# The value tiles, the output transposes and half B's stream of a hybrid encoder, laid out and ordered differently

## The chip, the core and the metric

The kernel runs on one core of a Trainium2 chip, all in float32. The core has a matrix engine (TensorE, PE in the rows, with its weight loads as PEld), a vector engine (VectorE, DVE), a scalar engine (ScalarE, ACT), GpSimd (POOL) and SyncE (SP). Each engine works through its own instructions in the order in which they were laid down at build time. Transfers (DMAs) are issued by SP and by ACT and run on 16 shared DMA engines. The metric is the device time of one execution in microseconds (us).

## What is computed

A sequence of 1024 tokens with 1024 channels passes two mixing layers, each followed by a SwiGLU block, and a final norm. The part that matters here is the second layer, an RWKV-7 recurrence with 16 heads of 64:

```
def step(state, inp):                       # for each token
    r_t, w_t, k_t, v_t, a_t, b_t = inp
    sa = einsum('bhvk,bhk->bhv', state, a_t)
    state = state * w_t + sa[..., None] * b_t + v_t[..., None] * k_t
    return state, einsum('bhvk,bhk->bhv', state, r_t)
...
y = group_norm(y) * ln_w + ln_b             # per head
y = (y + sum(r * k * r_k) * v) * g          # bonus, gate
h = h + y @ w_o
...
h = h + (silu(hn @ w_gate) * (hn @ w_up)) @ w_down     # SwiGLU, both layers
```

## The kernel before

**Halves and precision.** The tokens are worked on in two halves of 512, A (h = 0) and B (h = 1). A dense product of float32 precision is made of three matmuls on split operands (`mm3`, L393 to L395): a weight is loaded into a tile `raw` (ACT issues it, L121), ScalarE writes its rounded part `whi` (L157), VectorE writes the rest `wlo` (L158). There are three `raw` buffers, used in turn.

**Order.** Instructions are not issued in the order of the source. A planner at build time gives every engine a fixed list: it takes whatever is ready by its own clock, lowest priority number first, and a priority is the instruction's place in the source. `drive(dense, side, ratio)` walks a dense product and a side task together: each piece of dense work lets the side run for `ratio` times its weight, in the units that the side yields. The side's instructions are given a place 450 instructions earlier (`tc.high_priority(offset=AHEAD)`, AHEAD = 450).

**The recurrence.** `recur(h, wp)` works on 8 chunks of 64 tokens per half. It is the side task of a SwiGLU stage: `ffn(0, 1, ..., D0P[:3])` at a ratio of 6.2 for half A, `ffn(1, 0, ..., G1A[1])` at a ratio of 3 for half B. `with_reload` wraps it and adds the reload of the residual stream `h` in four loads of 512 KB. Its parts:
- `load(c)` fetches a chunk's operands on SP: `ar` (L1471), `bk` (L1473), the values into `uv` (L1476, L1477) and two pieces of the inverse into `XT` (L1483, L1486). Both `load(0)` and `load(1)` stand at the start.
- `uv` is a tile of 128 partitions by 8 by 2 by 64; for each head parity r the values of 64 tokens fill one half of the partitions, and `burst` later writes the solution u into the other half (L1573, L1574).
- `lnw`, the norm's gain, is spread to all partitions by two loads that ACT issues ahead of everything (L1446).
- `burst(c, ...)` makes the chunk's products with small matmuls through three PSUM buffers named `sm`. All of the recurrence's PE instructions are chained by `ordered` (L1456), so on PE they keep the order of the source.
- `post(jj)`, after each odd chunk, takes the pair's output `yp` out of PSUM into `ysb` (L1623), makes the group norm on VectorE, ScalarE and GpSimd, multiplies by `lnw` (L1661), adds the bonus `vch` (L1662), and leaves a function `turn_out` behind. It also loads `gch` (gate, L1626) and `vch` (L1629).
- `turn_out` transposes `ysb` on PE through two `sm` buffers (8 transposes), combines it with the gate on VectorE in 8 instructions (L1678) and stores it to `y_d` on SP (L1681). Before the change it is called inside the next chunk's `burst`, behind `flip_bk` and ahead of `load(c + 2)`; the last pair's is called at the end.

Between two bursts `recur` yields 12 units (BURST = 12), 6 of them ahead of `post`. When half A's recurrence is through, `y_d` is loaded again, split (tiles `ahi`, `alo`) and multiplied by `w_o` in `out_proj(0, ...)`.

**Half B's stream.** Ahead of the recurrence stands the down projection of layer 0. Its last products of the stage before end, and then `H[0]` (pool `ha0`) and `H[1]` (pool `hb0`) are reloaded from `hm_d` on SP (L1873): two loads for A, four for B, 512 KB each. A side task `wa1` waits 8 units and then prepares two small weights. The first residual additions of the stage are at L908, the others at L487. The hidden tiles of the stage before are stored by L737 (`hid_d`) and loaded again by L888 (`hd`).

Of the kernel before, what the change touches and what calls it, by code (L numbers as in the profile page):

```python
# [11 lines left out]
AF = mybir.ActivationFunctionType  # L12
# [4 lines left out]
P = 128  # L17
D = 1024
T = 1024
KT = D // P  # L20
# [10 lines left out]
BURST = 12.0  # L31
# [12 lines left out]
def tile_trunk(  # L44
# [8 lines left out]
    act, dve, pool, pe, sp = nc.scalar, nc.vector, nc.gpsimd, nc.tensor, nc.sync  # L53
# [25 lines left out]
    def bc(ap, shape):  # L79
        return ap.to_broadcast(shape)  # L80
# [204 lines left out]
    hm_d = [dram.tile([P, KT, HT], F32, name=f"hm_d{h}") for h in range(2)]  # L285
# [78 lines left out]
    H = [hA, hB]  # L364
# [198 lines left out]
    for h in range(2):  # L563
        ops = [mmt() for _ in range(4)]
        for kp in range(4):
# [4 lines left out]
            for kk in range(2):  # L570
                k = 2 * kp + kk
# [497 lines left out]
    rows = [slice(0, 64), slice(64, 128)]  # L1069
# [362 lines left out]
    def recur(h, wp):  # L1432
# [5 lines left out]
        def wt(tag, bufs, shape):  # L1438
            return wp.tile(shape, F32, tag=tag, bufs=bufs, name=tag)

        def smt():
            return pst("sm").rearrange("p (a b) -> p a b", b=64)

        lnw = wt("lnw", 1, [P, 8, 64])
        for r in range(2):
            act.dma_start(  # L1446
                lnw[rows[r]], rwkv_ln_w[0].rearrange("(p r d) -> r p d", r=2, d=64)[r].partition_broadcast(64)
            )
        C, ypair = {}, {}
        S, Q, last = [state_d], {}, []  # L1450

        def ordered(f, *args, **kw):

            if last:
                with tc.issue_after(last.pop()):
                    i = f(*args, **kw)  # L1456
            else:
                i = f(*args, **kw)
            last.append(i.ins)

        def mm(*args, **kw):
            ordered(pe.matmul, *args, **kw)

        def each(o, lhs, rhs):
            for p in range(8):
                for r in range(2):
                    mm(o[rows[r], p, :], lhs(r, p), rhs(r, p), start=True, stop=True)

        def load(c):
            ar = wt("ar", 2, [P, 8, 2, 64])  # L1470
            sp.dma_start(ar, ar_d[h][c])  # L1471
            bk = wt("bk", 1, [P, 8, 2, 64])
            sp.dma_start(bk, bk_d[h][c])  # L1473
            uv = wt("uv", 2, [P, 8, 2, 64])
            vs = v_d[h][c * 64 : c * 64 + 64]
            sp.dma_start(uv[64:128, :, 0, :], vs[:, 0])  # L1476
            sp.dma_start(uv[0:64, :, 1, :], vs[:, 1])  # L1477

            xx = wt("XT", 2, [P, 8, 96])
            x1, XT = xx[:, :, 0:32], xx[:, :, 32:96]  # L1480
            for r in range(2):
                b0 = r * 64
                sp.dma_start(  # L1483
                    xx[b0 : b0 + 32, :, 0:64], xi_d[h][0, :, r, c].rearrange("p i a j -> i p (a j)")
                )
                sp.dma_start(XT[b0 + 32 : b0 + 64, :, 32:64], xi_d[h][1, :, r, c, :, 1].rearrange("p i j -> i p j"))  # L1486
                pool.memset(XT[b0 + 32 : b0 + 64, :, 0:32], 0.0)
            gt = wt("gt", 2, [P, 8, 2, P])
            C[c] = (ar, bk, uv, gt, x1, XT)

        def gram(c, q):
            ar, bk, _, gt, _, _ = C[c]
            og = [pst("sm").rearrange("p (a b) -> p a b", b=P) for _ in range(2)]
            for j in range(4):
                p = q * 4 + j
                for b in range(2):
                    for r in range(2):
                        mm(
                            og[r][rows[b], j, :], bk[rows[r], p, b, :],
                            ar[rows[r], p].rearrange("p a b -> p (a b)"), start=True, stop=True,  # L1500
                        )
            for r in range(2):
                dve.tensor_tensor(
                    out=gt[:, q * 4 : q * 4 + 4, r, :], in0=og[r], in1=bc(gm.unsqueeze(1), [P, 4, P]), op=ALU.mult
                )
# [27 lines left out]
        def below2(c, w1):  # L1533
            XT = C[c][5]
            ox = smt()
            for p in range(8):
                for r in range(2):
                    b0 = r * 64
                    mm(
                        ox[b0 : b0 + 32, p, 0:32], w1[b0 + 32 : b0 + 64, p, :], XT[b0 + 32 : b0 + 64, p, 32:64],  # L1540
                        start=True, stop=True, tile_position=(b0 + 32, b0),
                    )
            act.activation(XT[0:32, :, 32:64], ox[0:32, :, 0:32], AF.Copy)
            dve.tensor_copy(XT[64:96, :, 32:64], ox[64:96, :, 0:32])

        def own(c):

            _, _, uv, gt, _, _ = C[c]
            ov = smt()
            for p in range(8):  # L1550
                for r in range(2):
                    mm(ov[rows[r], p, :], gt[rows[1 - r], p, r, 0:64], uv[rows[1 - r], p, r, :], start=True, stop=True)
            akv = wt("akv", 1, [P, 8, 64])
            act.activation(akv, ov, AF.Copy)
            return akv

        def burst(c, bkt, w1):

            ar, _, uv, gt, _, XT = C[c]
            cg, S0, more = h * 8 + c, S[0], c < 7  # L1560
            below2(c, w1)
            akv = own(c)
            oq = smt()
            each(oq, lambda r, p: ar[rows[r], p, 0, :], lambda r, p: S0[rows[r], p, :])
            Q = wt("Q", 1, [P, 8, 64])
            dve.tensor_tensor(out=Q, in0=akv, in1=oq, op=ALU.add)
            yield 0.1
            if more:
                gram(c + 1, 0)
                yield 0.1  # L1570
            ou = smt()
            each(ou, lambda r, p: XT[rows[r], p, :], lambda r, p: Q[rows[r], p, :])
            act.activation(uv[rows[0], :, 0, :], ou[rows[0]], AF.Copy)  # L1573
            dve.tensor_copy(uv[rows[1], :, 1, :], ou[rows[1]])  # L1574
            yield 0.1
            if c % 2 == 0:
                ypair[0] = psum["pool"].tile([P, 2, 8, 64], F32, tag="y", bufs=1, name="yp")

            yp = ypair[0][:, c % 2]
            for p in range(8):  # L1580
                for r in range(2):
                    mm(
                        yp[rows[r], p, :], ar[rows[r], p, 1, :], S0[rows[r], p, :], start=p == 0, stop=False,
                        skip_group_check=True,
                    )
            yield 0.1
            if more:
                gram(c + 1, 1)
                yield 0.1
            if cg < NCH - 1:  # L1590
                Sn = state_d if c == 7 else wt("S", 2, [P, 8, 64])
                os_ = smt()
                each(os_, lambda r, p: bkt[:, p, r * 64 : r * 64 + 64], lambda r, p: uv[:, p, r, :])
                tS = wt("Q", 1, [P, 8, 64])
                dve.tensor_tensor(out=tS, in0=S0, in1=os_, op=ALU.add)
                dve.tensor_tensor(out=Sn, in0=tS, in1=bc(pct[:, cg, :].unsqueeze(2), [P, 8, 64]), op=ALU.mult)
                S[0] = Sn
                yield 0.1
            for p in range(8):
                for r in range(2):  # L1600
                    mm(
                        yp[rows[r], p, :], gt[:, p, r, 64:128], uv[:, p, r, :], start=False, stop=p == 7,
                        skip_group_check=True,
                    )
            C.pop(c)
            yield 0.1
            if more:
                bkt = flip_bk(c + 1)
                if turned:
                    turned.pop()()  # L1610
                if c < 6:
                    load(c + 2)
                yield 0.1
                w1 = below(c + 1)
                yield 0.1
            return bkt, w1

        turned = []

        def post(jj):  # L1620
# [62 lines left out]
            turned.append(turn_out)  # L1683

        load(0)
        load(1)
        yield 0.2
        gram(0, 0)
# [3 lines left out]
        bkt = flip_bk(0)  # L1692
        w1 = below(0)
        yield 2.0
        for c in range(8):
            bkt, w1 = yield from burst(c, bkt, w1)
            yield BURST / 2
            if c % 2 == 1:
                yield from post(c // 2)
            yield BURST / 2  # L1700
        turned.pop()()
        yield 1.0

    early_o = {}

# [163 lines left out]
    prime_a()  # L1869
    for h, pl in ((0, ha_pool), (1, hb_pool)):  # L1870
        H[h] = pl.tile([P, KT, HT], F32, tag="h", name="h")
        for k in range(4 * (1 - h), KT, 2):
            sp.dma_start(H[h][:, k : k + 2, :], hm_d[h][:, k : k + 2, :])  # L1873

    def wa1():
        yield 8.0
        scale_wa1()

    drive(steps_a, wa1())
# [137 lines left out]
```

## Time and profile before

| | us |
|---|---|
| median of 3 runs | 2465.41 (2463.59 to 2466.77) |
| the profiled execution | 2461.21 |
| its span, first to last instruction | 2459.5 |
| PE busy | 2369.8 (96%) |
| VectorE busy | 1474.8 (60%) |
| ScalarE busy | 934.0 (38%) |
| mean granted TensorE clock | 0.990 of 2.4 GHz |

Times in the trace are counted from the span's first instruction. Half A's recurrence lies at about 1045 to 1263, half B's at about 1605 to 1845. In a row of the timeline, a bracket says how long the engine stood idle ahead of the instruction and what released it.

### The profile page before, as it was taken

What the parts mean: (1) busy time and instruction counts of PE and PEld (TensorE: products, weight loads), DVE (VectorE), ACT (ScalarE), POOL (GpSimd) and SP (SyncE); (2) the same over time, 40 slices, a digit from 0 to 9 for tenths busy, and PEclk for the clock granted to TensorE, in tenths of its full rate; (3) what the DMA queues carried; (4) which work ended last, traced back from release to release, by engine and by line L of the source; (5) the groups of instructions that cost most, each with busy time, mean ns of one, the idle gap of its engine ahead of it and who ended that gap; (6) DMA issues with size and microseconds to landing.
All of it is one profiled execution on the core that took longest, in us unless ns stands there. A gap on an engine that the chain in (4) does not pass through costs nothing.

```text
span 2459.5 us, 38177 instructions
## 1 busy us (share of the span) xinstructions
PE 2369.8 (96%) x15567; PEld 1942.6 (79%) x15567; DVE 1474.8 (60%) x2328; ACT 934.0 (38%) x1403; POOL 216.8 (9%) x246
## 2 busy tenths in 40 slices
PE   8999999999999999989999899988999999999998
PEld 6888888888787787778777688777888778888887
DVE  6445766665568758847668858845664446444443
ACT  6233444443125644323336644422332324222223
POOL 0200000000000033001100033100100001000001
PEclk9999999999999999999999999999999999999999
DMA  5114443334755554774445555784434322433231
GB/s 177 51 61 141 157 139 103 112 110 155 271 205 183 178 143 128 222 200 136 134 143 144 178 152 131 207 220 130 138 97 135 126 80 78 138 106 117 86 100 54
DMA packets 421103, 342.17 MB, mean 139 GB/s; under 512 B 94464, under 2 KB 368000, under 8 KB 420160
## 3 DMA queue, kind: packets, MB, share of 16 engines
q10 hardware_dynamic: 268160, 195.85, 26.4%
q1 hardware_dynamic: 152768, 143.89, 18.9%
q8 instruction: 122, 2.00, 0.3%
q14 instruction: 53, 0.43, 0.1%
HBM read 263.07 MB, written 76.61 MB: 138 GB/s over the span
## 4 chain that ended last, share of the span: by engine, by line
PE 77%; DVE 9%; DMA 7%; ACT 3%; issue 2%; POOL 1%; ACTq 1%; SPq 0%; POOLq 0%; DVEq 0%
PE mm L393 16%; PE mm L394 16%; PE mm L395 16%; PE mm L724 5%; PE mm L726 5%; PE mm L725 5%; PE sm L1456 5%; DVE wlo L158 1%; DMA raw<-in_ffn_w_down_dram 1%; DMA raw<-y_d 1%; PE yp L1456 1%; DVE h L487 1%; DVE mix L1163 1%; ACT whi L157 1%; PE aux L1377 1%
## 5 line engine op out<-in xcount | busy, mean ns | idle before, releaser
L393 PE MATMUL mm<-ahi,whi 128*128 128x512 f32 x1376 | 541.5, 394 | 5.3 <-DVE h L487 2.8
L394 PE MATMUL mm<-alo,whi 128*128 128x512 f32 x1376 | 542.2, 394 | 1.1 <-DVE alo L158 1.1
L395 PE MATMUL mm<-ahi,wlo 128*128 128x512 f32 x1376 | 540.6, 393 | 1.1 <-DVE wlo L158 1.1
L157 ACT ACTIVATE whi<-raw 128x1024 fp32r<-128x1024 f32 (+1 forms) x280 | 281.8, 1013 | 597.1 <-PE mm L394 448.6
L158 DVE TENSOR_TENSOR wlo<-raw,whi 128x1024 fp32r<-128x1024 f32 (+1 forms) x280 | 328.9, 1179 | 216.2 <-ACT whi L157 201.1
L393 PEld LDWEIGHTS mm<-ahi,whi 128*128 128x128 f32 x1376 | 259.2, 188 | 62.9 <-ACT whi L157 5.7
L395 PEld LDWEIGHTS mm<-ahi,wlo 128*128 128x128 f32 x1376 | 259.4, 189 | 57.7 <-issue 2.2
L394 PEld LDWEIGHTS mm<-alo,whi 128*128 128x128 f32 x1376 | 259.4, 189 | 57.5 <-issue 2.4
L487 DVE TENSOR_TENSOR h<-h,mm 128x512 f32<-128x512 f32 x276 | 185.1, 684 | 164.9 <-PE mm L395 156.7
L393 PE MATMUL mm<-hidhi,wdhi 128*128 128x512 f32 x304 | 117.2, 394 | 6.7 <-DVE h L487 3.6
L394 PE MATMUL mm<-hidlo,wdhi 128*128 128x512 f32 x304 | 119.0, 392 | 0.1
L395 PE MATMUL mm<-hidhi,wdlo 128*128 128x512 f32 x304 | 118.7, 391 | 0.0
L724 PE MATMUL mm<-ahi,whi 128*128 128x512 f32 x296 | 115.6, 390 | 0.0
L725 PE MATMUL mm<-alo,whi 128*128 128x512 f32 x296 | 115.2, 389 | 0.0
L726 PE MATMUL mm<-ahi,wlo 128*128 128x512 f32 x296 | 113.6, 389 | 0.0
L158 DVE TENSOR_TENSOR wdlo<-raw,wdhi 128x1024 fp32r<-128x1024 f32 x42 | 51.4, 1224 | 76.6 <-ACT wdhi L157 76.6
L949 DVE TENSOR_TENSOR sg<-sg,mm 128x512 f32<-128x512 f32 x52 | 35.7, 686 | 99.8 <-PE mm L395 99.6
L157 ACT ACTIVATE wdhi<-raw 128x1024 fp32r<-128x1024 f32 x42 | 44.3, 1058 | 134.7 <-DMA raw<-in_ffn_w_down_dram 100.0
L393 PE MATMUL mm<-hd,dhi 128*128 128x512 f32 x192 | 74.9, 391 | 4.1 <-DMA hd<-hid_d 2.4
L394 PE MATMUL mm<-hd,dhi 128*128 128x512 f32 x192 | 75.1, 391 | 0.0
L395 PE MATMUL mm<-hd,dlo 128*128 128x512 f32 x192 | 74.1, 389 | 0.0
L393 PEld LDWEIGHTS mm<-hidhi,wdhi 128*128 128x128 f32 x304 | 57.1, 188 | 21.3 <-DVE h L487 5.4
(395 smaller groups left out, 4282.7 us busy)
## 6 DMA issues: line engine op xcount, KB each, us to landing
raw<-in_ffn_w_down_dram ACTq DMA_DIRECT2D x88, 512.0 KB
raw<-in_ffn_w_gate_dram ACTq DMA_DIRECT2D x74, 512.0 KB
raw<-in_ffn_w_up_dram ACTq DMA_DIRECT2D x74, 512.0 KB
hid_d<-hid SPq DMA_DIRECT2D x36, 512.0 KB
hd<-hid_d SPq DMA_DIRECT2D x26, 512.0 KB
raw<-in_ab_w_in_dram ACTq DMA_DIRECT2D x16, 512.0 KB
raw<-in_ab_w_out_dram ACTq DMA_DIRECT2D x16, 512.0 KB
raw<-in_rwkv_w_r_dram ACTq DMA_DIRECT2D x16, 512.0 KB
```

The source lines that it names most:

```text
L157: act.activation(hi, src, AF.Copy)
L158: (eng or dve).tensor_tensor(out=lo, in0=src, in1=hi.bitcast(F32), op=ALU.subtract)
L393: pe.matmul(o, whi, xhi, start=first, stop=False)
L394: pe.matmul(o, whi, xlo, start=False, stop=False)
L395: pe.matmul(o, wlo, xhi, start=False, stop=last)
L487: dve.tensor_tensor(out=H[h][:, m, :], in0=H[h][:, m, :], in1=o, op=ALU.add)
L724: pe.matmul(o, wh[:, k, :], x[0][:, k, :], start=st, stop=False, skip_group_check=True)
L725: pe.matmul(o, wh[:, k, :], x[1][:, k, :], start=False, stop=False, skip_group_check=True)
L726: pe.matmul(o, wl[:, k, :], x[0][:, k, :], start=False, stop=k == 3, skip_group_check=True)
L949: dve.tensor_tensor(out=s, in0=s, in1=o, op=ALU.mult)
L1163: dve.scalar_tensor_tensor(out=t, in0=hn1[:, k, 0:HT], scalar=col(c), in1=t, op0=ALU.mult, op1=ALU.add)
L1456: i = f(*args, **kw)
```

## The change

Four edits. The values go into `uv` with the head parity outermost, so that each partition receives 2 KB in one piece where it received eight pieces of 256 bytes; the users of `uv` are re-indexed. The two loads of `lnw` move from ACT at the start of `recur` to SP, in the first chunk's burst behind `load(2)`. `turn_out` is called from the main loop, a quarter of BURST behind its own `post`, and no longer inside the next burst; `recur` no longer ends with a yield of its own. The four loads of half B's stream leave the place behind `prime_a()` and stand in `wa1`, after 2 units and then every 1.5 units; the small weights still follow at 8.

```diff
         lnw = wt("lnw", 1, [P, 8, 64])
-        for r in range(2):
-            act.dma_start(
-                lnw[rows[r]], rwkv_ln_w[0].rearrange("(p r d) -> r p d", r=2, d=64)[r].partition_broadcast(64)
-            )
...
-            uv = wt("uv", 2, [P, 8, 2, 64])
+            uv = wt("uv", 2, [P, 2, 8, 64])
             vs = v_d[h][c * 64 : c * 64 + 64]
-            sp.dma_start(uv[64:128, :, 0, :], vs[:, 0])
-            sp.dma_start(uv[0:64, :, 1, :], vs[:, 1])
+            sp.dma_start(uv[64:128, 0], vs[:, 0])
+            sp.dma_start(uv[0:64, 1], vs[:, 1])
...
-            act.activation(uv[rows[0], :, 0, :], ou[rows[0]], AF.Copy)
-            dve.tensor_copy(uv[rows[1], :, 1, :], ou[rows[1]])
+            act.activation(uv[rows[0], 0], ou[rows[0]], AF.Copy)
+            dve.tensor_copy(uv[rows[1], 1], ou[rows[1]])
...
                 bkt = flip_bk(c + 1)
-                if turned:
-                    turned.pop()()
                 if c < 6:
                     load(c + 2)
+                if c == 0:
+                    for r in range(2):
+                        sp.dma_start(
+                            lnw[rows[r]],
+                            rwkv_ln_w[0].rearrange("(p r d) -> r p d", r=2, d=64)[r].partition_broadcast(64),
+                        )
...
             yield BURST / 2
             if c % 2 == 1:
                 yield from post(c // 2)
-            yield BURST / 2
-        turned.pop()()
-        yield 1.0
+                yield BURST / 4
+                turned.pop()()
+                yield BURST / 4
+            else:
+                yield BURST / 2
...
         H[h] = pl.tile([P, KT, HT], F32, tag="h", name="h")
-        for k in range(4 * (1 - h), KT, 2):
-            sp.dma_start(H[h][:, k : k + 2, :], hm_d[h][:, k : k + 2, :])
+    for k in range(4, KT, 2):
+        sp.dma_start(H[0][:, k : k + 2, :], hm_d[0][:, k : k + 2, :])
 
     def wa1():
-        yield 8.0
+        yield 2.0
+        for k in range(0, KT, 2):
+            sp.dma_start(H[1][:, k : k + 2, :], hm_d[1][:, k : k + 2, :])
+            yield 1.5
         scale_wa1()
```

The users of `uv` in `own`, in the state's product and in the output's product read `uv[:, r, p, :]` where they read `uv[:, p, r, :]`; shapes and counts of instructions stay as they are.

## Rows read from the trace of the kernel before

**Rows 1.** The page: busy time, share and instructions of each engine.

```profile
PE 2369.8 (96%) x15567; PEld 1942.6 (79%) x15567; DVE 1474.8 (60%) x2328; ACT 934.0 (38%) x1403; POOL 216.8 (9%) x246
```

**Rows 2.** Windows: stretch, length, busy time of each engine, clock, DMA share, GB/s.

```profile
1050.00:1080.00 30.00, 22.53 (x244) 17.48 (x244) 10.51 (x15) 5.03 (x8) 0.00 (x0) 0.89 1.06 271
1600.00:1644.00 44.00, 37.15 (x236) 29.69 (x235) 19.81 (x31) 13.15 (x17) 0.00 (x0) 0.92 0.94 245
1698.00:1714.00 16.00, 8.54 (x63) 6.77 (x63) 7.20 (x14) 3.08 (x4) 0.00 (x0) 0.68 0.46 148
615.00:635.00 20.00, 15.04 (x55) 11.86 (x54) 10.38 (x14) 3.48 (x4) 0.00 (x0) 0.83 0.85 291
```

**Rows 3.** Windows: the work behind each stop that ran at a clock of 0.50.

```profile
1072.45:1076.40 3.95, 3.95 (x40) 2.85 (x40) 1.81 (x3) 0.81 (x2) 0.00 (x0) 0.50 1.13 267
1636.80:1642.60 5.80, 5.77 (x45) 4.60 (x46) 3.09 (x4) 2.60 (x4) 0.00 (x0) 0.50 1.15 284
1706.70:1711.60 4.90, 4.89 (x14) 4.03 (x15) 1.61 (x2) 2.02 (x3) 0.00 (x0) 0.50 0.30 107
627.30:633.00 5.70, 5.70 (x14) 4.44 (x15) 5.70 (x8) 0.00 (x0) 0.00 (x0) 0.50 0.93 324
```

**Rows 4.** Waits of the SP queue, whole span: us in total, times, longest.

```profile
SPq L1486 <- DMA lnw<-in_rwkv_ln_w_dram: 9.6, 2, 5.7
```

**Rows 5.** Timeline of SP, start of half A's recurrence: start, us, instruction.

```profile
1057.57 0.33 SPq L1486 DMA_DIRECT2D XT<-xi_d  x1
...
1059.42 1.59 SPq L1476 DMA_DIRECT2D uv<-v_d  x1
...
1068.52 0.57 SPq L1626 DMA_DIRECT2D gch<-g_d  x1
```

**Rows 6.** Timeline of ACT and PE, same stretch.

```profile
1071.81 1.08 ACT L1514 ACTIVATE bkt<-sm 128x512 f32<-128x512 f32 x2 [8.73 <-DMA h<-h_d]
1072.45 1.06 PE L1456 MATMUL sm<-XT,gt 32*32 32x32 f32 x32 [7.21 <-ACT bkt L1514]
```

**Rows 7.** Chain of waits, start of half B's recurrence: start, us, what.

```profile
1623.36 7.21 DMA uv<-v_d
```

**Rows 8.** Chain of waits, stretch 1680 to 1725.

```profile
1692.65 3.49 DMA raw<-in_ffn_w_down_dram
...
1698.52 5.21 DMA raw<-in_ffn_w_down_dram
```

**Rows 9.** DMA of 1092.9 to 1096.2: packets by size, SP's queue (q1).

```profile
DMA packets 954, 0.52 MB, mean 159 GB/s; under 512 B 879, under 2 KB 879, under 8 KB 953
...
q1 hardware_dynamic: 945, 0.49, 50.5%
```

**Rows 10.** DMA of 630 to 640: SP's queue.

```profile
q1 hardware_dynamic: 717, 2.60, 64.7%
```

**Rows 11.** DMA of 1052 to 1056: ACT's queue.

```profile
q10 hardware_dynamic: 1010, 0.33, 51.3%
```

**Rows 12.** Timeline around the first pair of half A.

```profile
1117.60 0.69 PE L1456 MATMUL sm<-XT,w 32*32 32x32 f32 x30
...
1122.76 0.69 DVE L1662 TENSOR_TENSOR ysb<-ysb,vch 128x512 f32<-128x512 f32 x1
...
1126.07 0.99 PE L1456 MATMUL sm<-ar,bk 64*64 64x128 f32 x27
```

**Rows 13.** Timeline: the split of half A's output, and its first product.

```profile
1284.24 1.22 DVE L158 TENSOR_TENSOR alo<-raw,ahi 128x1024 fp32r<-128x1024 f32 x1 [1.04 <-ACT ahi L157]
...
1290.13 0.50 PE L393 MATMUL mm<-ahi,whi 128*128 128x512 f32 x1 [0.37 <-ACT whi L157]
```

**Rows 14.** Timeline: start of the down projection.

```profile
615.55 2.07 SPq L1873 DMA_DIRECT2D h<-hm_d  x4
618.43 0.32 SPq L737 DMA_DIRECT2D hid_d<-hid  x1
...
626.54 1.28 DVE L908 TENSOR_TENSOR h<-ahi,mm 128x512 f32<-128x512 f32 x2 [8.13 <-DMA hid_d<-hid]
627.28 0.80 PE L393 MATMUL mm<-ahi 128*128 128x512 f32 x1 [4.96 <-DVE h L908]
```

More of the change, by code (lines that the diff above doesn't have):

```diff
@@ L1551, in own @@
                 for r in range(2):
-                    mm(ov[rows[r], p, :], gt[rows[1 - r], p, r, 0:64], uv[rows[1 - r], p, r, :], start=True, stop=True)
+                    mm(ov[rows[r], p, :], gt[rows[1 - r], p, r, 0:64], uv[rows[1 - r], r, p, :], start=True, stop=True)
             akv = wt("akv", 1, [P, 8, 64])
@@ L1592, in burst @@
                 os_ = smt()
-                each(os_, lambda r, p: bkt[:, p, r * 64 : r * 64 + 64], lambda r, p: uv[:, p, r, :])
+                each(os_, lambda r, p: bkt[:, p, r * 64 : r * 64 + 64], lambda r, p: uv[:, r, p, :])
                 tS = wt("Q", 1, [P, 8, 64])
@@ L1601, in burst @@
                     mm(
-                        yp[rows[r], p, :], gt[:, p, r, 64:128], uv[:, p, r, :], start=False, stop=p == 7,
+                        yp[rows[r], p, :], gt[:, p, r, 64:128], uv[:, r, p, :], start=False, stop=p == 7,
                         skip_group_check=True,
```

## The prediction

> **What bounds the kernel now.** I read the page first: PE is busy for 2369.8 of a span of 2459.5 us [rows 1], so it stands idle for 89.7 us, and VectorE, the next, has a third of its time free. The page also grants the full TensorE clock nearly throughout. PE is the bound, and a change that leaves PE's instructions as they are, as this one does, can only give back idle time and the slow matmuls behind it. So the second view was the windows, to see where PE stops near the edits. Four stretches stand out [rows 2]. In each, the length less PE's busy time is the idle time: 7.47 us at the start of half A's recurrence, 6.85 at the start of half B's, 7.46 behind half B's second chunk, 4.96 at the start of the down projection. Behind each stop PE works for some us at a clock of 0.50, the 1.2 GHz level, where the stretches around it have 1.00 [rows 3]: 3.95, 5.80, 4.90 and 5.70 us. Work at half the clock would have taken half the time, so the stops cost 1.98, 2.90, 2.45 and 2.85 us more. What is to be had is therefore 9.5, 9.8, 9.9 and 7.8 us, 37 us together, or 1.5%.
>
> **What ends these stops** I took from the chain of waits and the timelines. At half A's start the 16 DMA engines are full (share 1.06 [rows 2]). SP waits twice for `lnw` to land before it issues an `XT` load, 9.6 us in all, 5.7 the longer, so 3.9 the other [rows 4]. Behind that wait come `XT`, chunk 1's values (an issue took 1.59 us there [rows 5]) and then the stream of `h`. ScalarE stands for 8.73 us until a load of `h` lands, cannot empty `flip_bk`'s PSUM, and PE stands behind it for 7.21 us [rows 6]. At half B's start the chain goes through a load of `uv` that takes 7.21 us for 128 KB [rows 7]. At 1700 it goes through weight loads: one took 3.49 us, the next, issued beside chunk 3's operands, 5.21 [rows 8].
>
> **Values in rows of 2 KB.** I need the cost of a packet. Between 1092.9 and 1096.2 SP's queue had 50.5% of 16 engines for 3.3 us, 26.7 engine-us, for 945 packets, of which 879 of the window's 954 are small [rows 9]. In a stretch of large packets SP's queue took 64.7% of 160 engine-us, 103.5, for 717 packets of 2.60 MB: 144 ns for 3.6 KB [rows 10], so about 81 ns for 2 KB and 160 for 4 KB. The 66 large packets of the first window then cost 10.6, and 16.1 are left for 879 small ones: 18 ns each. One `uv` load, 512 packets, costs 9.2 engine-us and becomes 64 packets of 5.2. Four such loads stand at the start of each half, so 16 engine-us or 1.0 us of all engines is saved. ACT's queue, in another stretch, paid 51.3% of 64 engine-us for 1010 packets, mostly of 256 bytes [rows 11]: 32.5 ns each. By that price the four loads give 46 engine-us or 2.9 us. I keep both ends and take 1.5, nearer the first since it is SP's own queue. The Trainium skill (DMA: Bandwidth & Descriptors, section "Why small descriptors are slow (HBM only)") gives a 256-byte descriptor 11 cycles of which 3 are overhead; by it eight pieces of 88 cycles become one of 67, a quarter less, which as an estimate would make the four loads worth 0.55 us. The rows have 43% less even at the cheaper price, and I go by them.
>
> **The gain's load moved.** 1024 packets at 32.5 ns are 33 engine-us, 2.1 us of all engines, and they no longer fly while SP issues `XT`. They are not gone. A load that needs only a free buffer goes out when SP is free, whatever its place in the source: `gch` is issued at 1068.52 [rows 5], though its `post` stands behind two bursts, the first of which begins after 1072. So I expect `lnw` on SP right behind the stream of `h`, not at the end of the first burst. Its first reader is the first `ysb` by `lnw` product, some 50 us later, so it hides.
>
> **Sum for the two starts.** Half A: the SP wait of 3.9 us goes, the DMA time in front falls by 1.5 (values) and 2.1 (gain). They overlap, since the wait was a wait for those packets, so the landing that frees ScalarE comes between 1.5 us (only the values' bytes) and 7.2 us (the whole stop) earlier. I take 4.3, a little over the SP wait, and in proportion 1.2 of the 1.98 at half clock: 5.5. Half B's wait was 5.7 and its chain goes through `uv` itself; its stop is shorter and the `h` loads stay, so I take the same 5.5. Bounds 1.5 to 9.5 in A, 1.5 to 9.8 in B. Together 11.
>
> **The stop at 1700.** PE has neither weights nor recurrence there. A weight load beside the values should fall from 5.21 us towards 3.49: 1.7 at most. I take 1.5, and 1 for less time at half clock: 2.5, bounds 0 to 9.9.
>
> **The transposes moved.** Nothing is added on any engine: per pair 8 transposes, 8 VectorE products and a store, only earlier. Since PE keeps the recurrence's order, the next burst now stands behind the transposes, and these behind the `ysb` products. In half A's first pair the products end at 1123.45, while the next burst's first matmuls ran at 1117.6 [rows 12]: it starts 6 to 7 us later, with the transposes' 1.5 us between. But in the old order that burst then lay still until 1126.07 while VectorE finished the pair, and it carried the transposes in its middle. So most of the delay was already paid, and PE has dense work meanwhile. I book nothing, with bounds of 6 us gained and 15 lost (the rival below). The store and the gate's next load now meet `load(c + 2)`; the DMA share outside the starts is well below one (0.46 around 1700 [rows 2]), so they hide there.
>
> **Half B's stream.** Its four loads go out in a row at 615.55, ahead of the store of `hid` at 618.43, and VectorE waits 8.13 us, until 626.54, for a store of `hid` to land; PE then waits 4.96 [rows 14]. If the loads really came later, the store would land some 5 us sooner, and up to 7.8 us would be given back. But in the source the loads come after 2 to 6.5 units, and being a side task they count 450 instructions earlier. A unit is 24 matmuls and a few other instructions, so 6.5 units are some 200: they are ahead of even their old place. Like `gch`, they need only a buffer, so I expect them again at about 615, and book nothing.
>
> **Sum.** 5.5 + 5.5 + 2.5 = 13.5 us. The profiled execution took 2461.2 (the span and 1.7 around it), which becomes 2447.7. It lay 4.2 below the median of 2465.4; the difference carried to the median gives 2451.9, and I forecast 2452.
>
> **Rivals.**
> The stream does move (faster still). For it: the store and the four loads share the same engines, and the wait is in the rows. Against it: the priority counted above. It adds 4 to 7.8 us: 2444 to 2448.
>
> The stops only change their name (no change). ScalarE's 8.73 us was a wait for a load of `h` [rows 6], and those 2 MB per half stay; at 25 GB/s per engine (3.6 KB in 144 ns) they need 5 us of all 16 engines by themselves. If `lnw` behind them holds the next weight load instead, each start gives its 1.5 at most and 1700 nothing: 2462 to 2466. The Trainium skill (DMA: Bandwidth & Descriptors, section "Issuing engines are not separate DMA queues") says that DMAs of different issuers interleave on the same engines and that another issuer saves only its issue time; the share of 1.06 in rows 2 agrees.
>
> The recurrence becomes too long (slower). Each of half A's three middle pairs holds the next burst for 6 to 7 us; if the burst behind is no shorter for it, `y_d` is complete 20 us later. Its split ended at 1285.46 and `out_proj` began at 1290.13 [rows 13], so up to 4.7 us are free. Beyond that point PE has nothing else and loses the rest, about 15 us: with the starts' gain of 11 and 1700's 2.5 still there, it is level, and without them 2480. In half B the dense work lasts on past the recurrence, and nothing is lost. PE's program order is in the Trainium skill too (TensorE: Matmul & The Clock Gate, "Step-by-step: what each phase is for"): weight loads may be pulled ahead, matmuls stay in order. No run here has yet shown transposes waiting for `ysb`.
>
> **How the numbers follow.** Forecast (starts and 1700 shrink, stream unmoved): 45%. The same with the stream moved: 20%. Stops that change their name: 18%. Recurrence too long, or the planner laying the rest out worse: 17%, a few of them about level. The likeliest gives 2452, its own bounds 2444 to 2459. The range reaches from the faster rival's middle with some of the starts' upper bounds, 2439, to just above no change, 2468. This kernel can't tell less than 0.2%, about 5 us, from no change. Faster by more than that: 0.69, within: 0.16, slower: 0.15.
>
> **What would show it.** Right: no wait of SP for `lnw` ahead of `XT`; `lnw` issued behind the stream of `h`; `uv` issues of 0.3 us and under 512-byte packets down by 32 times 512, 16384; the idle time of 1050 to 1080 and 1600 to 1644 below 4 us each. Stream: the issues of L1873 still at the stop near 615. Transposes: within 3 us behind the last `ysb` product. Wrong: PE waiting for `ysb` at the transposes, an `out_proj` later than half A's dense work, or ScalarE again standing at the starts for a load of `h`.

## The result, and the profile after

The changed kernel took 2473.81 us (median of 11, 2469.43 to 2477.5), the kernel before, on the same chips, 2465.41 (2458.81 to 2471.17): a ratio of 1.0034, 95% interval 1.0026 to 1.0042. It is slower by 8.4 us; 2452 was forecast, with a range up to 2468. Its profiled execution has a span of 2471.8 us, 12.3 more than the one of before; that one lay 4.2 us below its kernel's median.

The page: the engines' busy time, as in [rows 1], and the packets.

```profile
PE 2383.2 (96%) x15567; PEld 1953.6 (79%) x15567; DVE 1474.7 (60%) x2328; ACT 934.2 (38%) x1403; POOL 218.7 (9%) x246
...
DMA packets 406767, 342.17 MB, mean 138 GB/s; under 512 B 78080, under 2 KB 351616, under 8 KB 405824
```

The instructions are as many as before. PE's busy time is 13.4 us longer, so its matmuls ran slower: the mean granted clock is 0.981 for 0.990. Windows: the first two and the last answer to the first, second and fourth of [rows 2] (the second lies 13.59 us later, like half B here), the third is half A's end, the fourth the end of half B's recurrence.

```profile
1050.00:1080.00 30.00, 25.11 (x249) 19.55 (x249) 11.12 (x16) 5.03 (x8) 0.00 (x0) 0.89 1.01 278
1613.59:1657.59 44.00, 39.39 (x321) 31.76 (x321) 22.07 (x34) 14.63 (x20) 0.00 (x0) 0.96 0.97 264
1273.35:1312.42 39.07, 20.32 (x53) 13.83 (x54) 28.62 (x46) 15.75 (x27) 1.43 (x2) 0.65 0.56 178
1800.00:1860.00 60.00, 55.59 (x680) 45.71 (x679) 33.92 (x69) 20.58 (x34) 3.57 (x2) 0.94 0.36 107
615.00:635.00 20.00, 15.01 (x55) 11.87 (x54) 10.38 (x15) 3.48 (x4) 0.00 (x0) 0.83 0.82 290
```

The starts' stops shrink, to 4.89 and 4.61 us from 7.47 and 6.85. The stop at 615 stands as it was. The third row is the loss: PE works 20.32 of 39.07 us, at a mean granted clock of 0.65. In the kernel before the same stretch, and the one that answers to the fourth row (13.59 us earlier), hold

```profile
1273.35:1312.42 39.07, 36.56 (x159) 28.63 (x159) 26.81 (x35) 16.88 (x23) 2.15 (x2) 1.00 0.70 218
1786.41:1846.41 60.00, 60.00 (x631) 49.72 (x630) 38.78 (x81) 20.86 (x36) 5.65 (x2) 1.00 0.36 109
```

so at half A's end 16.2 us of work are missing, and a part of the rest ran at the 1.2 GHz level (clock 0.50 from 1289.98 to 1295.08). What stands at half A's end, by the timeline of the changed kernel:

```profile
1272.96 0.39 PE L395 MATMUL mm<-hd,wlo 128*128 128x512 f32 x1
...
1276.99 0.30 PE L1452 MATMUL sm<-ident,ysb 128*128 128x128 f32 x1 [3.65 <-DVE ysb L1662]
...
1278.20 1.73 PE L1452 MATMUL sm<-ident,ysb 128*128 128x128 f32 x7 [0.90 <-DVE ysb L1662]
...
1281.30 0.54 SPq L1681 DMA_DIRECT2D y_d<-gch  x1
...
1288.87 1.06 ACT L157 ACTIVATE ahi<-raw 128x1024 fp32r<-128x1024 f32 x1 [12.33 <-DMA raw<-y_d]
...
1289.98 0.80 PE L393 MATMUL mm<-ahi,whi 128*128 128x512 f32 x1 [4.41 <-ACT ahi L157]
...
1301.60 0.49 PE L393 MATMUL mm<-ahi,whi 128*128 128x512 f32 x1 [2.60 <-ACT ahi L157]
1303.58 0.79 PE L393 MATMUL mm<-ahi,whi 128*128 128x512 f32 x1 [1.49 <-ACT whi L157]
```

The dense work ends at 1273.35. PE then waits for the last pair's `ysb`, transposes it, and waits again until `y_d` has been stored, loaded and split. `out_proj` begins at 1289.98, 16.6 us after the dense work, and goes on in pieces until 1308. Before, it followed the dense work at once:

```profile
1283.92 0.40 PE L395 MATMUL mm<-hd,wlo 128*128 128x512 f32 x1
1284.15 0.39 PE L393 MATMUL mm<-ahi,whi 128*128 128x512 f32 x1
```

So the product at 1290.13 in [rows 13] is not its first, as the heading there says: it is the first that waits for the split of the next weight. From the first product to that one lie 6.0 us before and 13.6 now (to 1303.58).

The dense work itself ends 11 us sooner than before (1273.35 for 1284.3). The windows from half A's last two stores of `xi_d` to that end, before and then after:

```profile
1042.93:1284.32 241.39, 225.90 (x3224) 185.43 (x3223) 150.91 (x309) 74.83 (x131) 22.92 (x20) 0.99 0.53 150
1043.26:1273.35 230.09, 224.12 (x3215) 184.81 (x3213) 145.97 (x297) 71.08 (x124) 23.69 (x20) 0.99 0.51 147
```

PE runs the same matmuls in both but for the last pair's eight transposes, and stands idle for 15.5 us before and for 6.0 now; 2.5 of the difference lie at the start. With the transposes put back (e1 below) it is 13.9. The moved transposes thus gave PE some 8 us up to there, and took more behind it.

Why the last pair is late shows in the first (it answers to [rows 12]):

```profile
1120.27 0.69 DVE L1662 TENSOR_TENSOR ysb<-ysb,vch 128x512 f32<-128x512 f32 x1
...
1123.67 0.28 PE L1452 MATMUL sm<-ident,ysb 128*128 128x128 f32 x1
...
1126.71 0.69 PE L1452 MATMUL sm<-XT,w 32*32 32x32 f32 x32
...
1133.94 0.99 PE L1452 MATMUL sm<-ar,bk 64*64 64x128 f32 x27
```

The `ysb` products end at 1120.96, 2.5 us sooner than before, and the transposes follow at 1123.67. But the next burst's first products (`XT` by `w`) run at 1126.71, where they ran at 1117.60 [rows 12], and its products of `ar` by `bk` at 1133.94, where they ran at 1126.07: 8 us late. Behind the second and the third pair these products are 19 and 24 us late; some of it is made up between the pairs, and 18 are left at the last store.

SP's timeline at half A's start answers to [rows 5]:

```profile
1056.91 0.45 SPq L1472 DMA_DIRECT2D uv<-v_d  x1
...
1063.41 0.43 SPq L1482 DMA_DIRECT2D XT<-xi_d  x1
1065.54 0.80 SPq L1782 DMA_DIRECT2D h<-h_d  x2
1066.38 1.32 SPq L1609 DMA_DIRECT2D lnw<-in_rwkv_ln_w_dram  x2
```

`lnw` goes out right behind the stream of `h`, and no wait of SP for it is left. ScalarE's stand answers to [rows 6]:

```profile
1069.38 1.08 ACT L1510 ACTIVATE bkt<-sm 128x512 f32<-128x512 f32 x2 [8.88 <-DMA XT<-xi_d]
```

It is as long as before (8.73), only 2.4 us earlier, and is now a wait for `XT`.

### The profile page after: what moved, and what is told of

It reads as the page before. It is cut to its first block, busy times and chain, and to the rows that moved or that the text cites. A ratio compares the mean times of both kernels' runs of the same rounds, so it can differ in the third digit from the quotient of the medians.

```text
span 2471.8 us, 38174 instructions
## 1 busy us (share of the span) xinstructions
PE 2383.2 (96%) x15567; PEld 1953.6 (79%) x15567; DVE 1474.7 (60%) x2328; ACT 934.2 (38%) x1403; POOL 218.7 (9%) x246
## 2 busy tenths in 40 slices
DMA packets 406767, 342.17 MB, mean 138 GB/s; under 512 B 78080, under 2 KB 351616, under 8 KB 405824
## 4 chain that ended last, share of the span: by engine, by line
PE 77%; DVE 9%; DMA 7%; ACT 3%; issue 2%; POOL 2%; SPq 0%; ACTq 0%; POOLq 0%; DVEq 0%
PE mm L393 16%; PE mm L394 16%; PE mm L395 16%; PE sm L1452 5%; PE mm L724 5%; PE mm L726 5%; PE mm L725 5%; DMA raw<-in_ffn_w_down_dram 2%; DVE wlo L158 1%; PE yp L1452 1%; DVE h L487 1%; DMA raw<-y_d 1%; DVE mix L1163 1%; PE aux L1377 1%; PE mm L574 1%
```

## The experiments

Each kernel is the whole program with one part of the change undone, done alone or altered. The table gives the ratio to the kernel before with its interval, and times from each profiled execution. Half A is counted from the start of its last two stores of `xi_d` (one row of the timeline; L1414 in both kernels): to the last store of half A's `y_d`, to the first store of its norm behind `out_proj` (`n_d`, L462), to the same two stores of half B. "Half B" is from there to the end of the span. Each time is that of one execution. Before and e12 have the engines' instructions in the same order and differ by 0.7 us at `y_d`, 3.2 in half A and 1.4 in half B, so differences of that size are not read.

| run | ratio | y_d | n_d | half A | half B |
|---|---|---|---|---|---|
| before | 1 | 219.9 | 312.7 | 561.6 | 854.9 |
| changed | 1.0034 (1.0026, 1.0042) | 238.0 | 326.6 | 574.9 | 853.7 |
| e1 all transposes back | 0.9966 (0.9952, 0.9979) | 217.3 | 310.5 | 560.8 | 851.8 |
| e2 transposes alone | 1.0055 (1.0038, 1.0072) | 244.1 | 333.9 | 583.3 | 856.9 |
| e3 moved in half B alone | 0.9932 (0.9916, 0.9948) | 216.2 | 310.7 | 562.0 | 845.6 |
| e4 e1, stream late | 0.9959 (0.9946, 0.9973) | 216.7 | 311.4 | 560.3 | 845.4 |
| e5 values alone | 0.9953 (0.9939, 0.9967) | 219.5 | 313.6 | 564.7 | 847.0 |
| e6 gain's load alone | 0.9985 (0.9975, 0.9995) | 215.8 | 312.2 | 561.3 | 855.8 |
| e7 moved in half A alone | 0.9999 (0.9985, 1.0014) | 238.0 | 326.1 | 573.7 | 843.9 |
| e8 untied | 1.0004 (0.9992, 1.0015) | 236.5 | 326.1 | 575.1 | 846.5 |
| e9 changed, 4 buffers | 1.0004 (0.9993, 1.0015) | 222.4 | 313.2 | 562.8 | 855.5 |
| e10 e1, 4 buffers | 1.0039 (1.0025, 1.0053) | 202.5 | 317.7 | 565.9 | 861.4 |
| e11 untied, y's buffer | 1.0023 (1.0012, 1.0035) | 236.1 | 326.4 | 574.8 | 851.2 |
| e12 stream alone | 0.9998 (0.9988, 1.0009) | 219.2 | 312.6 | 564.8 | 856.3 |
| e13 e1, GpSimd splits | 0.9977 (0.9966, 0.9988) | 216.7 | 309.1 | 557.9 | 853.6 |
| e14 changed, GpSimd splits | 1.0056 (1.004, 1.0072) | 237.6 | 325.8 | 575.6 | 860.8 |
| e15 e3, GpSimd splits | 0.9946 (0.9928, 0.9963) | 216.5 | 311.5 | 559.5 | 848.3 |

**Which part loses, and where.** e1 puts the transposes back, e2 moves them alone:

```diff
                 bkt = flip_bk(c + 1)
+                if turned:
+                    turned.pop()()
...
-                yield BURST / 4
-                turned.pop()()
-                yield BURST / 4
+                yield BURST / 2
```

> The changed kernel with the transposes of a pair put back into the next chunk's products; values in 2 KB rows, the gain's late load and the stream's edit stay. Theory T (the moved transposes lengthen half A's recurrence, whose end has almost no slack, and nothing else loses): the last store of y_d of half A falls back by about 18 us, out_proj starts when the dense work ends, the start of half A keeps its gain of some 8 us and half B's start its 2; 2450 to 2458, ratio to the kernel before 0.994 to 0.997. Rival P (the other edits make the planner lay the work out worse and the transposes are innocent): at most 0.2% from the changed kernel, ratio 1.001 to 1.005. Rival L (both share the loss): ratio 0.998 to 1.001.

> The kernel before with only the transposes moved. Theory T: no gain at the starts, y_d of half A complete some 20 us later than in the kernel before, out_proj 16 to 22 us later; 2478 to 2490, ratio 1.005 to 1.010, more than the whole change costs. Rival P: ratio 0.998 to 1.002. Rival L: 1.002 to 1.004.

e3 and e7 take the new place in one half only (`if c % 2 == 1 and h == 1`, or `h == 0`):

> The changed kernel with the transposes moved in half B alone, in the old place in half A. Theory T: half B's dense work lasts on past its recurrence, so the longer recurrence there costs at most 3 us; 2450 to 2460, ratio 0.994 to 0.998, within 3 us of the run with both put back. Rival (a longer recurrence costs the same in either half): 2465 to 2475, ratio 1.000 to 1.004.

> The changed kernel with the transposes moved in half A alone, in the old place in half B. Theory T with the last runs' sizes (the move costs 20 to 25 us in half A, where the recurrence sets when out_proj can begin, and gives some 8 in half B): 2478 to 2488, ratio 1.004 to 1.008, so slower than the whole change. Rival (what half B gave was not the move, but a different layout of that one run): 2470 to 2476, ratio 1.001 to 1.0035, as the whole change.

The column of half A separates cleanly: with the transposes moved there (changed, e2, e7) it stands at 573.7 to 583.3 us, without (e1, e3) at 560.8 and 562.0. The move costs 12 to 14 us in half A with the other edits in, 21.7 without them (e2 against before; e2's profile is its slowest execution, 8.3 us above its median, so this is rather too much). That is theory T for half A, and e2's total (2480.61) lies where T put it. The other totals do not follow it alone. e1 is 0.34% faster, at the weak end of T's ratios and 2.7 us over its range of times. e3, expected within 3 us of e1, is 10.6 us under it (2450.03 and 2460.66), and e7, expected at 1.004 to 1.008, is level with before, since its half B took 843.9 us. Half B is a question of its own, below.

**Whether lateness of `y_d` is the loss.** e9 leaves the change whole and shortens the recurrence by another means; e10 is its control.

```diff
-    MIXED = {"mm": ("mm", 3), "aux": ("sm", 3), "sm": ("sm", 3)}
+    MIXED = {"mm": ("mm", 2), "aux": ("sm", 4), "sm": ("sm", 4)}
```

> The changed kernel, whole, with four PSUM buffers for the recurrence and two for the dense products (three and three before), so that the recurrence is shorter by another means: in PE's order of instructions the last pair's transposes stand 72 dense matmuls earlier (about 16 us), 12 behind their place in the kernel before. Theory T (half A loses only because y_d is late for out_proj): the stretch from half A's last store of xi_d to half B's falls from 574.9 us to within 4 of that of the next run; 2450 to 2464. Rival (the move costs by itself, or two dense buffers cost more than they save): it stays at 570 or more, 2468 to 2480.

> The control of that run: four and two PSUM buffers, transposes in the old place. What two buffers for the dense products cost or what the shorter recurrence gives is seen here: the stretch from xi_d to xi_d was 560.8 us with three and three. Theory T: y_d is complete 24 us sooner and gains nothing by it, since out_proj waits for the dense work: 558 to 564, total 2452 to 2464. Rival (two buffers hold the dense products): over 570, total over 2470.

With `y_d` at 222.4 us, near where it was before, half A is back at 562.8: 12.1 us of the loss are gone while the transposes stay moved. (The total, 2466.33, is 2 above T's range.) The edit also moved the other end: the dense work lasts until 1286.89 here, 13.5 us later than in the changed kernel, and `out_proj` follows it at once. The windows of e9, against the changed kernel's third row above:

```profile
1273.35:1312.42 39.07, 36.17 (x152) 28.67 (x153) 24.91 (x33) 16.45 (x23) 1.23 (x2) 0.96 0.74 213
```

PE is nearly full there again. e10's `y_d` comes 14.8 us sooner than e1's and gains nothing. Its half A takes 5.1 us more, and there PE's dense products wait 10.2 us for the sums of `h` on VectorE, 4.5 in e1, which fits two buffers being too few. Its half B takes 9.6 more, but there PE waits for the recurrence's own copies (`uv`, `w`), and e9's half B is only 1.8 over the changed kernel's, so this part is not explained. e10 missed its total. In the kernels traced here `out_proj` begins 8.6 to 9.2 us behind the last store of `y_d` (changed, e2, e7, e8, e11) or with the end of the dense work (before, e1, e3, e9, e10), whichever is later: 246.7 us for a `y_d` of 238.0 and a dense end of 230.1 in the changed kernel, 248.4 for 202.5 and 248.6 in e10. What `y_d` gains ahead of the dense work's end is worth nothing, what is late behind it counts.

**What holds the next burst.** e8 unties the transposes from the recurrence's chain of matmuls:

```diff
-                        ordered(
-                            pe.transpose, o[:, i * P : (i + 1) * P],
+                        pe.transpose(
+                            o[:, i * P : (i + 1) * P],
```

> The changed kernel with the transposes moved, but not tied into the recurrence's order of matmuls: the next burst may overtake them. Theory C (that tie makes the next burst wait until the ysb products are done): the burst starts some 10 us sooner in each of half A's pairs, out_proj when the dense work ends; 2448 to 2460, ratio 0.993 to 0.997. Theory K (the two PSUM buffers which the transposes take from the recurrence's three hold the burst as well): 2468 to 2476, ratio 1.000 to 1.004, with bursts hardly sooner than in the changed kernel.

e11 does so too and writes them into the pair's own PSUM tile:

```diff
-                    o = pst("sm")
+                    o = yb[:, q].rearrange("p a b -> p (a b)")
```

> The changed kernel with the transposes untied from the recurrence's order and written into the pair's own PSUM buffer of y, no longer into the recurrence's three. Theory K (those three are handed out in the order of the source, so the burst behind asks in vain until the transposes have begun): the burst's first products (XT by w, gt by uv) run some 10 us sooner than in the changed kernel, before the transposes; but its products for y now wait for the buffer, half A's last y_d comes at most 3 us sooner; 2462 to 2472, ratio 0.999 to 1.003. Rival (tie and buffers were all that held it): y_d 15 us sooner, 2448 to 2458.

PE's timeline in e8, then in e11:

```profile
1123.48 0.38 PE L1670 MATMUL sm<-ident,ysb 128*128 128x128 f32 x2
1123.79 0.37 PE L1452 MATMUL sm<-XT,w 32*32 32x32 f32 x10
```

```profile
1116.00 0.69 PE L1452 MATMUL sm<-XT,w 32*32 32x32 f32 x30
...
1123.57 0.27 PE L1671 MATMUL yp<-ident,ysb 128*128 128x128 f32 x1
...
1133.65 1.08 PE L1452 MATMUL yp<-S,ar 64*64 64x64 f32 x29
```

Untied, the burst still begins only when the transposes have begun; half A keeps its loss. With the recurrence's PSUM tiles left to the burst, its first products stand at 1116.0, as before the change, but its products for `y` stand behind the transposes, which now use the pair's tile, and run at 1133.65. VectorE has read that tile by 1129.0; PE does dense products from there on. So the place behind the pair is held by the recurrence's tiles and then by `yp`, and taking away the tie and the tiles brings `y_d` 1.9 us. That the tie by itself would hold the burst too no run shows. That the tiles are handed out in the order of the source is what fits; e11 shows only that the burst is free once the transposes take none of them.

**The edits at the starts.** e5 and e6 do one each on the kernel before, as in the diff of the change.

> The kernel before with only the values in rows of 2 KB. The change without the moved transposes gave 8.4 us (ratio 0.9966). Theory U (the bytes and packets of the values bind at the starts): this edit gives about half of it, 3 to 5 us, ratio 0.998 to 0.9988. Rival W (the wait of SP for the gain's load was the stop, the values' packets hid behind it): under 1.5 us, ratio 0.9994 to 1.0005.

> The kernel before with only the gain's load moved from ScalarE's queue ahead of the recurrence to SP's queue behind the first chunk. Theory U: the other half, 3 to 5 us, ratio 0.998 to 0.9988. Rival W: nearly all of the 8.4 us, ratio 0.9965 to 0.9975. Rival N (ScalarE waits for the loads of h, whatever flies before them): under 1.5 us.

In half A `y_d` comes 0.4 us sooner with the values alone, 4.1 with the gain's load alone, 2.6 to 3.7 with both (e1, e3, e4). PE's stop there says the same: 7.2 us before (7.0 in e12), 8.0 with the values alone, 5.6 with the gain's load alone, 4.7 and 3.9 with both (changed, e1). So in half A it was SP's wait and not the packets, which is rival W's cause, though not its total. The totals point the other way, 11 us for the values and 3 for the gain; but 7.9 of e5's 11 lie in half B, and its half A is no shorter than before. The two do not add up to the 8.4 of e1's ratio either, and why e5's half B is shorter is open.

**The stream.** e12 takes its edit alone; e4 orders the loads behind the store on SP, on top of e1:

```diff
+            with tc.issue_after(hid_stored[0]):
                 sp.dma_start(H[1][:, k : k + 2, :], hm_d[1][:, k : k + 2, :])
```

> The kernel before with only half B's stream of h put into steps. Every theory: the four loads are issued at 615 as before, and PE's and SP's instructions stand in the same order; ratio 0.999 to 1.001. A ratio outside would say how much two layouts of the same order differ.

> As the run with the transposes put back, and half B's four loads of h ordered behind the last store of hid on SP's queue, so that they can no longer go out at 615. Theory S (the stop at 626 is the store waiting for bytes of these loads): the store lands 4 to 6 us sooner, PE's stop of 5.0 us near 622 to 627 nearly vanishes with its slow matmuls, 4 to 8 us less than the run with the transposes put back. Rival (the store itself is slow, or the loads that wait for it are late next): under 1.5 us of difference.

e12 is the control that it should be. In e4 SP issues the store first, and VectorE's sum that waits for it runs at 620.79, 5.8 us sooner than in [rows 14]. PE's waits there:

```profile
PE mm L393 <- DMA hd<-hid_d: 9.0, 1, 9.0
```

The stop moves from 627 to 635 and grows from 4.96 us [rows 14] to 9.0: late next is a load of `hid`, issued at 621.99 behind the loads of `h`. Theory S falls; e4's interval overlaps e1's.

**Half B.** e1, e4 and e7 have the same source of half B and take 851.8, 845.4 and 843.9 us. The changed kernel and e3 have one source of it too and take 853.7 and 845.6. The largest stop that differs lies behind the second chunk: 5.28 us in e1, none above 1.1 in e7. VectorE in the kernel before, where it is 6.20, then in e7:

```profile
1704.84 1.23 DVE L158 TENSOR_TENSOR wdlo<-raw,wdhi 128x1024 fp32r<-128x1024 f32 x1 [5.03 <-ACT wdhi L157]
1705.98 0.68 DVE L1595 TENSOR_TENSOR Q<-S,sm 128x512 f32<-128x512 f32 x1
```

```profile
1701.74 1.29 DVE L1499 TENSOR_TENSOR gt<-sm,gm 128x512 f32<-128x512 f32 x2 [0.49 <-PE sm L1452]
1702.94 0.68 DVE L1591 TENSOR_TENSOR Q<-S,sm 128x512 f32<-128x512 f32 x1
```

In the first, a split of a down weight whose load is late stands ahead of the recurrence's `Q`; in the second no split does. e13 to e15 give these splits of half B to GpSimd.

```diff
+        if key[:3] == ("d", 1, 0) and any(key[3] in g for g in G1A[1]):
+            split(view(raw), view(hi), view(lo), pool)
```

> As the run with all transposes put back (851.8 us from half B's last store of xi_d to the end), and in half B's mixed stretch the split of the down projection's weights is made by GpSimd, no longer by VectorE. Theory V (half B differs from run to run of the same source because VectorE stands, in order, at a split that waits for a weight's load, with the recurrence's Q or gt behind it): the stop of 7.0 us behind half B's second chunk falls below 2.5, the stretch to 844 to 848, total 2450 to 2456. Rival (the load itself is late for whoever needs it next): the stop stays or moves to the down products, 850 or more, total as before it, 2458 to 2463.

> The changed kernel, whole, with the same splits on GpSimd in half B. Theory V: half A keeps its loss (574 to 576 us from store to store), and half B's stops of 4.0 and 4.4 us go: 844 to 849 in place of 853.7, total 2464 to 2468, ratio 0.999 to 1.001. Rival: 2470 to 2476.

> The fastest so far (transposes moved in half B alone, ratio 0.9932) with the same splits on GpSimd. Its half B had a stop of 1.6 us where the others had 4 to 7.6. Theory V: little left to gain, 843 to 846 us of half B in place of 845.6, ratio 0.992 to 0.9945, and within 3 us of the run with all put back and the splits on GpSimd, since the place of the transposes then matters to half B no more. Rival (the moved transposes themselves speed half B up): 6 us or more ahead of that run.

Theory V falls with e13 and e14; e15 lies 8.3 us under e13, as its rival said. What is late is the weight's load, as e13's rival had it. The stand moves to ScalarE, which makes the other half of the split; in e13 PE waits 3.18 and 1.24 us for its `bkt` behind the second chunk (the profile puts 2.83 us of that `bkt`'s delay down to GpSimd's split), in e14 `ysb` stands behind a late weight. ScalarE and PE in e14:

```profile
1809.47 1.06 ACT L160 ACTIVATE wdhi<-raw 128x1024 fp32r<-128x1024 f32 x1 [6.09 <-DMA raw<-in_ffn_w_down_dram]
1810.44 1.06 ACT L1626 ACTIVATE ysb<-yp 128x512 f32<-128x512 f32 x2
```

```profile
1822.71 0.45 PE L1455 MATMUL sm<-ident,ysb 128*128 128x128 f32 x1 [9.09 <-ACT ysb L1657]
```

The moved transposes make PE stand 9.09 us there. What the move is worth in half B stays open: with half A in the old place it went with gains (e3 against e1 6.2 us, e15 against e13 5.3), with half A moved with losses (changed against e7 9.8, and e14 against e13, which differ in half A too, 7.2). Kernels with one source of half B differ by more than that: e14 and e15 by 12.5 us, the changed kernel and e3 by 8.1, e1 and e7 by 7.9. In the traces the engines' instructions of half B stand in another order in each of these pairs; that the order makes the difference is not shown.

## Why the prediction was wrong, point by point

**The step that failed** is "The transposes moved": "most of the delay was already paid, and PE has dense work meanwhile. I book nothing". The first half did not hold. The burst that lay still until 1126.07 [rows 12] had done its first half (`XT`, `gt`, `Q`) while VectorE finished the pair. Behind the transposes that half comes after the pair, so the delay is not paid but added: `y_d` is complete 18.1 us later (238.0 for 219.9). The second half held only while there was dense work: until 1273.35 PE stood idle 6.0 us where it had stood 15.5, and mainly for that reason the dense work ran out 11 us sooner. Then PE stood. Half A lost 13.3 us in the profiles (574.9 for 561.6). Of the 22 us between forecast and result, some 17 are the move (ratio 1.0034 for 0.9966 in e1), the other 5 are gains that were booked too high.

**The rival that was right** is the recurrence that becomes too long, in mechanism and place: `y_d` "20 us later" (18.1), PE loses "about 15" (16.2 us of work missing, 13.9 us at `n_d`). It had 17%, together with a worse layout by the planner. That its price came out is in part luck. Its slack of 4.7 us rests on a misreading of [rows 13]: `out_proj` began at 1284.15, right behind the dense work. By the 8.7 us from `y_d` to `out_proj` in the changed kernel, `y_d` could have come some 12 us later at no cost (an estimate: 241.2 less 219.9 and 8.7). The 11 us by which the dense work ended sooner, which the rival did not foresee, took that slack away. `out_proj` then began 5.5 us later against the stores of `xi_d` (246.7 for 241.2), and another 7.6 were lost in its first block, at late pieces of `y_d` and late weights. Its total was put at level with the gains or at 2480 without them; the starts gave less than half of theirs, and 2474 lies between. The Trainium skill (TensorE: Matmul & The Clock Gate, "Step-by-step: what each phase is for") says that matmuls stay in program order, which speaks for this rival. The trace agrees as far as it goes: PE stood 3.65 and 0.90 us at the transposes for `ysb`, and no other matmul ran meanwhile.

**The starts** were mis-sized. Half A's stop shrank by 2.58 us and its slow stretch not at all (0.89 in both windows), for 5.5 booked; half B's by 2.24 (clock 0.96 for 0.92), for 5.5. The values' packets gave nothing that can be seen in half A: 0.4 us of `y_d` (e5), for 1.5 booked. The Trainium skill (DMA: Bandwidth & Descriptors, "Why small descriptors are slow (HBM only)") had led to an estimate of 0.55 us; e5 can't tell that from nothing. An issue of `uv` took 0.45 us at the least and not 0.3. ScalarE's stand kept its 8.9 us under another name, as the second rival had it.

**The stop at 1700** did change: 4.0 us of it remain, and a new one of 3.8 us stands at 1826, within the fourth window above, where PE had no idle time before. The two weight loads in its chain took 4.12 and 4.65 us for 3.49 and 5.21, as much together as before, so no load got shorter by what was booked. What the prediction had not named is that the recurrence's product stands behind the split of that weight, in VectorE's order. 2.5 were booked, next to nothing was gained: half B took 853.7 for 854.9.

**Half B's stream**: booked at nothing, right (e12 0.9998). But the price named for really moving it, up to 7.8 us, was wrong: e4 made the stop longer.

**The shown signs**: under 512-byte packets down by 16384 (94464 to 78080), `lnw` behind the stream, the loads of `h` at 615, transposes 2.7 us behind the last `ysb` product, all as written. The idle time at the starts is 4.89 and 4.61, not below 4. Two of the three signs of being wrong came: PE waiting for `ysb`, and `out_proj` later than the dense work. ScalarE stood as well, but for `XT` and not for `h`.

**A faster kernel** came out: e3, everything but half A's move, 2450.03 us, ratio 0.9932 (0.9916 to 0.9948). How much of it is chance in half B is open, as said.

## What to carry to other kernels

Before moving work to an earlier place in an in-order engine, ask what ran in the gap that it now fills: a chain that lay still in its middle may have used its first half to hide the work behind which it is now put. A side chain beside dense work costs nothing until the dense work ends, and whatever lets the dense work run without stops brings that end nearer; count the slack against the new end. And compare stages, not totals alone: kernels that differ in half A alone differed by 7.9 to 12.5 us in half B (e1 and e7, e14 and e15).

## What the runs showed that I had not expected

Kernels with one source of a stage differ by up to 12.5 us in it (e14 and e15, half B), more than the whole change. In the long stops of half B that were read (6.20 us before, 9.09 in e14), the engine that stands is the one that has a late weight load's split in front of the recurrence, VectorE or, relieved of it, ScalarE. A store put ahead of four 512 KB loads let the sum that waits for it run 5.8 us sooner, and the reader behind those loads then stood for 9.0 us (e4). And a recurrence given one PSUM buffer more, with one fewer for the dense products, ended 14.8 us sooner (e10), while half A as a whole took 5.1 us longer.
